# Storing attention operands whole and splitting them after the load, with one row spread moved from DRAM to the tensor engine

## The chip, the cores and the metric

The kernel runs on one core of a Trainium2 chip. The metric is the device time of one execution in microseconds (us). Before the change the median of three runs was 2708.47 us (2705.57 to 2710.37).

A core has TensorE (matrix products, transposes), VectorE (DVE), ScalarE (ACT) and GpSimd (POOL), each with its own queue worked off in order, and SyncE (SP), whose queue issues nearly all transfers here. The transfers themselves run on 16 DMA engines. PEld is TensorE's loading of weights.

## The reference

An encoder of two layers over 1024 tokens of width 1024, all in float32. In each layer one input projection feeds four groups of four heads, whose outputs are joined, projected and added to `x`; then comes an MLP with squared ReLU.

```
proj = rms_norm(x, norm1_g) @ w_in                       # split into the inputs of A, B, C, D
A: q = rms_norm(cq) @ w_uq ; c = rms_norm(ckv) ; k, v = c @ w_uk, c @ w_uv    # rotary part of 32, shared key
   o = softmax(q k^T * 96**-0.5) v                        # dense, 4 heads
B: w = softmax(q1 k1^T) - lam * softmax(q2 k2^T) ; o = rms_norm(w v)          # dense, 4 heads
C: o = softmax(q k^T / 8 over |i - j| <= 128, with sink) v                    # banded, 4 heads on 2 key heads
D: o = softmax(q k^T / 8 + bias over 8 rows x 16 columns) v                   # neighbourhood, 4 heads
x = x + concat(norm(A), B, norm(C), norm(D)) @ w_out
x = x + square(relu(rms_norm(x) @ w_up)) @ w_down
```

## The kernel before

Activations are held transposed: 8 tiles of 128 features by 1024 tokens. To keep float32 accuracy from products of the reduced type `fp32r`, an operand is **split** into a high part (a ScalarE copy to `fp32r`) and a low part (the operand minus the high part, on VectorE or GpSimd; `split`, line 190 for the subtraction, 196 for the copy). A product then takes three matmuls: high by high, high by low, low by high (lines 222 to 224).

A layer's attention (`attention`) goes in order through B, D, C and A, with other work woven in by `weave`: beside B run the latent projections (`proj_latent`) and D's projections (`proj_d`); beside D run C's projections (`proj_c`) and then the second step of the latents (`latent_up`), which gives A's queries, keys and values; beside C and A runs the first half of the output projection. An order of priorities is written out this way, and a planner with a simulated timeline turns it into each engine's queue; on the chip each queue then runs in order.

Between a projection and its attention all operands go through DRAM. A projected half tile (128 features by 512 tokens) comes out of PSUM into a buffer `part` (three of them), scaled by the norm's reciprocals; rotary tiles (`ev_rope`) take two such buffers, D's (`ev_grid`, which reorders the tokens into column blocks) take two per tile. `emit_parts` then splits it into `both` (two buffers, high and low side by side), by ScalarE and by VectorE or, from the second tile of B on, GpSimd, and SP stores both parts. Values (`to_values`) are first transposed by TensorE, and the split reads PSUM: ScalarE copies the high part and VectorE subtracts.

The attention loads what it needs into `stack` buffers (128 by 1024; eight share one pool) and values into `v` (two buffers, `vtile`, high and low side by side, so that one matmul gives both products). B puts high, high and low parts of a query on 3 x 32 partitions against high, low, high of the key, so that one matmul does the three products. D and C put the high and the low part of the query on the two halves of the partitions, against a stack with the key's high part twice and one with its low part twice. A has four stacks a head: high and low, of query and key, each of 64 plain and 32 rotary rows. Softmax takes score tiles from PSUM on VectorE (lines 812, 1058, 1089: add bias or mask, negate, running minimum), then an exponential on ScalarE into `p` tiles (six buffers), then transposes (846, 991), another split into `pth` and `ptl`, and the products with `v` (834, 835, 1003, 1004). The denominators' reciprocals are turned into a row by a transpose, stored to DRAM (`drows`, `rows_of`), and loaded back spread over the partitions (`rz`, `spread`); GpSimd or VectorE multiplies.

The reciprocal norms of the latents go the same way: `proj_latent` ends with `rows_of`, and `latent_up` begins with two `spread` loads, into `rq` and `rkv`. Elsewhere, `spread_here` makes such a spread without DRAM: for each 128 tokens a matmul of the broadcast column with the identity (line 299), and a VectorE copy out of PSUM (294).

D's bias table has six blocks of 128 keys a head: three for a query block inside, and three for the edges, where no column mask on one side is needed.

Of the kernel before, what the change touches and what calls it, by code (L numbers as in the profile page):

```python
# [78 lines left out]
def neighbours():  # L79

    a = np.arange(P)
    q, k = a[:, None], a[None, :]
    r, c, rk, ck = q // 8, q % 8, k // 8, k % 8
    start = np.clip(r - 4, 0, 8)
    row_ok = (rk >= start) & (rk <= start + 7)
    out = np.full((P, 6, P), -1)
    for slot, ok in enumerate((row_ok & (ck >= c), row_ok, row_ok & (ck < c), row_ok, row_ok, row_ok)):
        at = (rk - r + 7) * 31 + 8 * (slot % 3 - 1) + ck - c + 15  # L90
        out[:, slot] = np.where(np.broadcast_to(ok, (P, P)), at, -1)
    return out
# [55 lines left out]
class Trunk:  # L148
# [232 lines left out]
    def attention(self, l):  # L381
# [208 lines left out]
    def ev_rope(self, tabs, dst):  # L590

        dst = dst.rearrange("a g f h s -> a (g f) h s")

        def ev(n, ps):
# [6 lines left out]
            self.tt(t1, t1, t2, ALU.add, self.eng)  # L601
            self.emit_parts(t1, [(dst[:, :, h, sl].rearrange("a p s -> p a s"), slice(h * 64, h * 64 + 64))
# [31 lines left out]

    def to_values(self, dst, tag="mm"):
# [3 lines left out]
        def then(n, y):  # L639
# [6 lines left out]
            nc.scalar.activation(v[..., 0:64], src, AF.Copy)  # L646
            self.tt(v[..., 64:128], src, v.bitcast(F)[..., 0:64], ALU.subtract)
            self.keep(dst[:, :, n * 4:n * 4 + 4].rearrange("h p k e -> p h (k e)"), b.bitcast(F))
# [16 lines left out]
    def proj_latent(self, l, one, xs, rb, tabs, lat, krd, rows_out):  # L665
# [10 lines left out]
        def ev(n, ps):  # L676
# [18 lines left out]
        rows_out.append(self.rows_of(self.rsqrt_cols(both, 192)))  # L695
        yield True

    def latent_up(self, l, lat, rows, qa, ka, va):
        nc, d = self.nc, self.d
        rq, rkv = self.big_tile(F, "rq"), self.big_tile(F, "rkv")  # L700
        self.spread(rq, rows[0], 0, 2)
        self.spread(rkv, rows[0], 1, 2)
# [32 lines left out]
        yield from two(w1[2:3], parts[2:3], plain(rkv, kn[:, 0]))  # L735
# [3 lines left out]
        yield from two([w1[0], both(w1[1])], parts[0:2], plain(rq, qn[:, 1]))  # L739
        yield from two(w1[3:4], parts[2:3], plain(rkv, kn[:, 1]))  # L740
# [190 lines left out]
    def attn_a(self, l, qa, kn, krd, va, ys):  # L931
# [3 lines left out]
        def head(h):  # L935
# [563 lines left out]
```

## Time and profile before

| | |
|---|---|
| Median of three runs | 2708.47 us (2705.57 to 2710.37) |
| The profiled execution's own time | 2709.95 us |
| Its span, first to last instruction | 2707.9 us |
| TensorE busy | 2549.6 us, 94% |
| VectorE, ScalarE, GpSimd busy | 1943.0, 1439.8, 1130.9 us (72, 53, 42%) |
| Mean granted TensorE clock | 0.969 |
| DMA | 389.19 MB in 186931 packets, 144 GB/s on average |

Attention takes roughly the first 650 us of each layer, the MLP the rest. Busy time counts an instruction from its start to its end; the granted clock is the share of full speed at which TensorE was let run. A group of instructions is shown as output and inputs by the program's names, shape, count, then busy time and mean of one in ns, then the idle time of its engine just before and what ended it. Helpers put many operations on one line (190, 196), so the names tell them apart.

### The profile page before, as it was taken

The page shows a single profiled execution, that of the slowest core. Times are in us where ns is not written, and L with a number is a line of the kernel's source. Part 1 is how long each engine was busy: PE and PEld are TensorE (multiplying, and loading weights), DVE is VectorE, ACT ScalarE, POOL GpSimd, SP SyncE. Part 2 cuts the span into 40 slices and gives each one's busy share as a digit, 9 for nine tenths or more (in the row PEclk, how much of TensorE's full clock was granted, in tenths as well). Part 3 has the DMA queues.
Part 4 walks back from the last instruction along what each step waited for, and adds up shares of the span by engine and source line. Part 5 has one row for each costly group of instructions (what it writes and reads, how often), then busy time and mean ns, then how long its engine had stood idle before and what let it go on. Part 6 is the DMA issues. An engine that isn't in the chain of part 4 may idle for free.

```text
span 2707.9 us, 37502 instructions
## 1 busy us (share of the span) xinstructions
PE 2549.6 (94%) x12296; PEld 2112.5 (78%) x12296; DVE 1943.0 (72%) x3379; ACT 1439.8 (53%) x2601; POOL 1130.9 (42%) x754
## 2 busy tenths in 40 slices
PE   8989988999899998999999999889998999999997
PEld 6778876787778887888877788668876788878886
DVE  6777866774966668887567777677749666688775
ACT  4667756664534444444436776566635344444444
POOL 2555642201345554545434656321013455544442
PEclk9989988999999999999998899899999999999998
DMA  5534597222144457444244446962221444664431
GB/s 175 169 107 129 158 287 239 82 89 63 46 144 148 153 170 267 143 142 141 95 139 134 121 113 183 295 202 69 71 71 52 154 153 152 221 221 146 136 105 63
DMA packets 186931, 389.19 MB, mean 144 GB/s; under 512 B 23712, under 2 KB 26736, under 8 KB 186736
## 3 DMA queue, kind: packets, MB, share of 16 engines
q1 hardware_dynamic: 172912, 361.62, 43.2%
q10 hardware_dynamic: 13824, 25.17, 2.7%
q8 instruction: 97, 1.59, 0.2%
q14 instruction: 98, 0.80, 0.1%
HBM read 263.29 MB, written 123.41 MB: 143 GB/s over the span
## 4 chain that ended last, share of the span: by engine, by line
PE 73%; DVE 12%; DMA 6%; ACT 4%; issue 3%; POOL 1%; SPq 0%; DVEq 0%; ACTq 0%; POOLq 0%
PE u L222 8%; PE u L224 8%; PE u L223 8%; PE mm L222 5%; PE mm L223 5%; PE mm L224 5%; PE p L222 5%; PE p L223 5%; PE p L224 5%; PE sb L810 3%; PE tr L846 3%; DVE p L812 2%; DVE part L190 2%; PE pv L835 2%; PE pv L834 2%
## 5 line engine op out<-in xcount | busy, mean ns | idle before, releaser
L190 POOL TENSOR_TENSOR wl<-raw,wh 128x512 fp32r<-128x512 f32 x448 | 632.8, 1413 | 704.8 <-ACT wh L196 691.0
L196 ACT ACTIVATE wh<-raw 128x512 fp32r<-128x512 f32 x448 | 281.5, 629 | 576.2 <-PE u L223 310.9
L190 POOL TENSOR_TENSOR wl<-ws,wh 128x512 fp32r<-128x512 f32 (+1 forms) x112 | 147.3, 1316 | 461.0 <-ACT wh L196 436.1
L222 PE MATMUL u<-far,wh 128*128 128x512 f32 x768 | 301.8, 393 | 11.4 <-ACT ev L1242 8.3
L224 PE MATMUL u<-far,wl 128*128 128x512 f32 x768 | 300.6, 391 | 2.2 <-POOL wl L190 2.2
L190 DVE TENSOR_TENSOR raw<-raw 128x512 f32<-128x512 f32 x256 | 223.1, 877 | 109.1 <-POOL wl L190 55.6
L223 PE MATMUL u<-far,wh 128*128 128x512 f32 x768 | 300.6, 391 | 0.0
L190 DVE TENSOR_TENSOR ptl<-tr,pth 128x512 fp32r<-128x512 f32 (+2 forms) x384 | 238.3, 629 | 68.5 <-ACT pth L196 66.8
L815 ACT ACTIVATE p<-p,nm 128x1024 f32<-128x1024 f32 x192 | 220.2, 1147 | 92.3 <-DVE nm L812 91.6
L196 ACT ACTIVATE pth<-tr 128x512 fp32r<-128x512 f32 (+2 forms) x384 | 205.2, 546 | 108.5 <-PE tr L846 64.9
L222 PE MATMUL p<-far,wh 128*128 128x512 f32 x640 | 252.9, 395 | 7.5 <-DVE ev L190 7.5
L224 PE MATMUL p<-far,wl 128*128 128x512 f32 x640 | 251.5, 393 | 1.5 <-POOL wl L190 1.5
L223 PE MATMUL p<-far,wh 128*128 128x512 f32 x640 | 252.2, 394 | 0.0
L810 PE MATMUL sb<-stack 96*128 96x512 f32 x640 | 217.5, 422 | 22.1 <-DVE nm L812 21.4
L190 DVE TENSOR_TENSOR far<-act,far 128x512 fp32r<-128x512 f32 x224 | 207.3, 955 | 14.7 <-ACT far L196 14.7
L190 POOL TENSOR_TENSOR p<-p 128x1024 f32<-128x1024 f32 x64 | 154.0, 2411 | 129.6 <-ACT p L898 121.3
L222 PEld LDWEIGHTS u<-far,wh 128*128 128x128 f32 x768 | 145.3, 189 | 43.5 <-ACT ev L1242 9.1
L222 PE MATMUL mm<-xh,wh 128*128 128x512 f32 x416 | 170.9, 411 | 0.8 <-DVE part L190 0.3
L224 PEld LDWEIGHTS u<-far,wl 128*128 128x128 f32 x768 | 145.2, 189 | 33.5 <-POOL wl L190 3.0
L812 DVE CUSTOM_DVE_ANT_0 p<-sb,zero,nm 128x512 f32<-128x512 f32 x192 | 142.4, 743 | 37.7 <-PE sb L810 34.6
L223 PEld LDWEIGHTS u<-far,wh 128*128 128x128 f32 x768 | 145.4, 189 | 30.0
L223 PE MATMUL mm<-xl,wh 128*128 128x512 f32 x416 | 167.7, 403 | 0.0
(245 smaller groups left out, 6110.1 us busy)
## 6 DMA issues: line engine op xcount, KB each, us to landing
act<-acts SPq DMA_DIRECT2D x224, 256.0 KB
raw<-in_w_up SPq DMA_DIRECT2D x128, 256.0 KB
acts<-ev SPq DMA_DIRECT2D x128, 256.0 KB
raw<-in_w_down SPq DMA_DIRECT2D x128, 256.0 KB
acts<-ev ACTq DMA_DIRECT2D x96, 256.0 KB
ws<-in_w_in SPq DMA_DIRECT2D x76, 256.0 KB
rz<-drows SPq DMA_DIRECT2D x40, 256.0 KB
stack<-kd SPq DMA_DIRECT2D x32, 256.0 KB
```

The lines of the kernel that those rows point to most:

```text
L190: (eng or self.nc.vector).tensor_tensor(out=out, in0=a, in1=b, op=op)
L196: nc.scalar.activation(hi, src, AF.Copy)
L222: mm(ps, w[0], x[0][:, sl], start=start, stop=False)
L223: mm(ps, w[0], x[1][:, sl], start=False, stop=False)
L224: mm(ps, w[1], x[0][:, sl], start=False, stop=stop)
L810: self.nc.tensor.matmul(ps, q[:, qt * P:(qt + 1) * P], k[:, sl], start=i == 0, stop=i == len(passes) - 1)
L812: self.nc.vector.tensor_tensor_reduce(out=p[:, sl], in0=ps, in1=self.zero[:, 0:1].bitcast(F).broadcast_to([P, 512]), scale=-scale, scalar= ...
L815: self.nc.scalar.activation(p, p, AF.Exp, bias=nm[:, 1:2], scale=-1.0, accum_out=z)
L834: nc.tensor.matmul(out, v[:, kt], h[:, sl], start=kt == 0, stop=False)
L835: nc.tensor.matmul(out, v[:, kt], lo[:, sl], start=False, stop=kt == 7)
L846: nc.tensor.transpose(t[:, k * 256 + i * P:k * 256 + (i + 1) * P], p[:, (j * 2 + k) * P:(j * 2 + k + 1) * P], self.ident)
```

## The change

The operands of A, C and D, except the queries of C and D, are stored as they are, in half the bytes, and so are all values; B's queries and keys are stored split as before.

- `to_whole` stores the `part` buffer of a plain tile; `ev_rope` does the same where its target has no axis for the two parts; `proj_latent` stores the shared rotary key from its buffer.
- `to_values` copies the transposed values out of PSUM on ScalarE into a `part` buffer and stores that. `vtile` loads the whole values into half of a `p` buffer and splits them into `v`.
- `split_here` splits a loaded stack: ScalarE copies the high part to a second stack, VectorE subtracts in place. A splits the query and the key of each head (96 by 1024), D each head's key and C each key head's key (128 by 1024). The number of stacks does not change.
- `proj_latent` keeps the latents' reciprocals as a column; `latent_up` spreads them with two `spread_here` calls.
- D's bias table has five blocks; the query blocks at the edges read two blocks that are two apart.

```diff
-    out = np.full((P, 6, P), -1)
-    for slot, ok in enumerate((row_ok & (ck >= c), row_ok, row_ok & (ck < c), row_ok, row_ok, row_ok)):
-        at = (rk - r + 7) * 31 + 8 * (slot % 3 - 1) + ck - c + 15
+    out = np.full((P, 5, P), -1)
+    for slot, (off, ok) in enumerate(((-1, row_ok), (-1, row_ok & (ck >= c)), (0, row_ok),
+                                      (1, row_ok & (ck < c)), (1, row_ok))):
+        at = (rk - r + 7) * 31 + 8 * off + ck - c + 15
...
-        qb, kb, vb = dr([2, 2, 4, 16, 2, S], "qb"), dr([2, 2, 4, 16, 2, S], "kb"), dr([4, P, 8, P], "vb")
-        qd, kd, vd = dr([2, 2, P, S], "qd"), dr([2, 2, P, S], "kd"), dr([4, P, 8, P], "vd")
-        qc, kc, vc = dr([2, 2, 2, 32, 2, S], "qc"), dr([2, 2, 32, 2, S], "kc"), dr([2, P, 8, P], "vc")
-        lat, krd = dr([2, 3, P, S], "lat"), dr([2, 16, 2, S], "krd")
-        qa = dr([2, 2, P, S], "qan"), dr([2, 4, 16, 2, S], "qar")
-        ka, va = dr([2, 2, P, S], "kan"), dr([4, P, 8, P], "va")
+        qb, kb, vb = dr([2, 2, 4, 16, 2, S], "qb"), dr([2, 2, 4, 16, 2, S], "kb"), dr([4, P, 8, 64], "vb")
+        qd, kd, vd = dr([2, 2, P, S], "qd"), dr([2, P, S], "kd"), dr([4, P, 8, 64], "vd")
+        qc, kc, vc = dr([2, 2, 2, 32, 2, S], "qc"), dr([2, 32, 2, S], "kc"), dr([2, P, 8, 64], "vc")
+        lat, krd = dr([2, 3, P, S], "lat"), dr([16, 2, S], "krd")
+        qa = dr([2, P, S], "qan"), dr([4, 16, 2, S], "qar")
+        ka, va = dr([2, P, S], "kan"), dr([4, P, 8, 64], "va")
...
-                yield from one(T_DK[t], xs, self.ev_grid(rb, self.to_parts(kd[:, t])))
+                yield from one(T_DK[t], xs, self.ev_grid(rb, self.to_whole(kd[t])))
...
+            if whole:
+                for h in range(2):
+                    self.keep(dst[:, h, sl], t1[h * 64:h * 64 + 64])
+                return
             self.emit_parts(t1, [(dst[:, :, h, sl].rearrange("a p s -> p a s"), slice(h * 64, h * 64 + 64))
...
+    def to_whole(self, dst):
+
+        def then(n, y):
+            self.keep(dst[:, n * 512:n * 512 + 512], y)
+        return then
...
-            src = ps.rearrange("p (k h d) -> p h k d", k=4, h=2)
-            b = self.both()
-            v = b.rearrange("p h (k e) -> p h k e", k=4)
-            nc.scalar.activation(v[..., 0:64], src, AF.Copy)
-            self.tt(v[..., 64:128], src, v.bitcast(F)[..., 0:64], ALU.subtract)
-            self.keep(dst[:, :, n * 4:n * 4 + 4].rearrange("h p k e -> p h (k e)"), b.bitcast(F))
+            v = self.part()
+            nc.scalar.activation(v.rearrange("p (h k d) -> p h k d", h=2, k=4),
+                                 ps.rearrange("p (k h d) -> p h k d", k=4, h=2), AF.Copy)
+            self.keep(dst[:, :, n * 4:n * 4 + 4].rearrange("h p k d -> p h (k d)"),
+                      v.rearrange("p (h e) -> p h e", h=2))
...
-            self.emit_parts(y[64:112], [
-                (krd[:, :, h, sl].rearrange("a p s -> p a s"), slice(64 + 32 * h, 80 + 32 * h))
-                for h in range(2)], slice(64, 112))
+            for h in range(2):
+                self.keep(krd[:, h, sl], y[64 + 32 * h:80 + 32 * h])
...
-        rows_out.append(self.rows_of(self.rsqrt_cols(both, 192)))
+        r = self.col("rlat", 16)
+        nc.vector.tensor_copy(r, self.rsqrt_cols(both, 192))
+        out.append(r)
...
-        self.spread(rq, rows[0], 0, 2)
-        self.spread(rkv, rows[0], 1, 2)
+        self.spread_here(rq, rows[0][:, 0:8])
+        self.spread_here(rkv, rows[0][:, 8:16])
...
-        plain = lambda r, dst: self.ev_plain(r, self.to_parts(dst))
-        yield from two([w0[2], both(w0[3])], parts[0:2], plain(rq, qn[:, 0]))
+        plain = lambda r, dst: self.ev_plain(r, self.to_whole(dst))
+        yield from two([w0[2], both(w0[3])], parts[0:2], plain(rq, qn[0]))
...
+    def split_here(self, hi, v):
+
+        self.nc.scalar.activation(hi, v.bitcast(F), AF.Copy)
+        self.tt(v, v.bitcast(F), hi.bitcast(F), ALU.subtract)
+
     def vtile(self, src):
+
         v = self.ap.tile([P, 8, P], R, tag="v", bufs=2, name="v")
-        self.load(v.bitcast(F), src)
+        raw = self.ptile()[:, 0:512].rearrange("p (k d) -> p k d", k=8)
+        self.load(raw, src)
+        self.split(v[..., 0:64], v[..., 64:128], raw)
         return v
...
-            for nope, rope in (((qn[0, t], qr[0, h])), (kn[0, t], krd[0]),
-                               (qn[1, t], qr[1, h]), (kn[1, t], krd[1])):
-                s = self.stack()
+            for nope, rope in ((qn[t], qr[h]), (kn[t], krd)):
+                hi, s = self.stack(), self.stack()
                 self.load(s.bitcast(F)[0:64], nope[h2 * 64:(h2 + 1) * 64])
                 self.load(s.bitcast(F)[64:96], run(rope))
-                tl.append(s[0:96])
-            qh, kh, ql, kl = tl
+                self.split_here(hi[0:96], s[0:96])
+                tl += [hi[0:96], s[0:96]]
+            qh, ql, kh, kl = tl
...
                     self.load(qs.bitcast(F)[half], qd[i, t, rows])
-                    self.load(ks[0].bitcast(F)[half], kd[0, t, rows])
-                for i in range(2):
-                    self.load(ks[1].bitcast(F)[i * 64:(i + 1) * 64], kd[1, t, rows])
+                    self.load(ks[1].bitcast(F)[half], kd[t, rows])
+                self.split_here(*ks)
...
-                    b0 = {0: 4, 7: 3}.get(i, 0)
-                    w = ps.shape[1]
+                    near = bias[:, {0: slice(2, 5, 2), 7: slice(0, 3, 2)}.get(i, slice(1, 4))]
+                    blocks = lambda t: t.rearrange("p (a b) -> p a b", b=P)
...
-                        out=p, in0=ps, in1=bias[:, b0:b0 + w // P].rearrange("p a b -> p (a b)"),
+                        out=blocks(p), in0=blocks(ps), in1=near,
...
-            for n, k in enumerate(ks):
-                for i in range(2):
-                    self.load(k.bitcast(F)[i * 64:(i + 1) * 64], run(kc[n, kv]))
+            for i in range(2):
+                self.load(ks[1].bitcast(F)[i * 64:(i + 1) * 64], run(kc[kv]))
+            self.split_here(*ks)
```

More of the change, by code (lines that the diff above doesn't have):

```diff
@@ L590, in ev_rope @@
     def ev_rope(self, tabs, dst):
-        dst = dst.rearrange("a g f h s -> a (g f) h s")
+        whole = len(dst.shape) == 4
+        dst = dst.rearrange("g f h s -> (g f) h s" if whole else "a g f h s -> a (g f) h s")
         def ev(n, ps):
@@ L663, in latent_parts, with proj_latent @@
                         slice(0, rows), g[:rows])
-    def proj_latent(self, l, one, xs, rb, tabs, lat, krd, rows_out):
+    def proj_latent(self, l, one, xs, rb, tabs, lat, krd, out):
         nc = self.nc
@@ L731, in latent_up @@
         yield from two([w0[0], both(w0[1])], parts[0:2], self.ev_rope(tabs, qr))
-        plain = lambda r, dst: self.ev_plain(r, self.to_parts(dst))
-        yield from two([w0[2], both(w0[3])], parts[0:2], plain(rq, qn[:, 0]))
+        plain = lambda r, dst: self.ev_plain(r, self.to_whole(dst))
+        yield from two([w0[2], both(w0[3])], parts[0:2], plain(rq, qn[0]))
         w1 = self.weights(d["w_lat"][l, 1])
-        yield from two(w1[2:3], parts[2:3], plain(rkv, kn[:, 0]))
+        yield from two(w1[2:3], parts[2:3], plain(rkv, kn[0]))
         w2 = self.weights(d["w_lat"][l, 2])
@@ L738, in latent_up @@
             yield from two(w2[t:t + 1], parts[2:3], self.ev_plain(rkv, self.to_values(va[2 * t:2 * t + 2])))
-        yield from two([w1[0], both(w1[1])], parts[0:2], plain(rq, qn[:, 1]))
-        yield from two(w1[3:4], parts[2:3], plain(rkv, kn[:, 1]))
+        yield from two([w1[0], both(w1[1])], parts[0:2], plain(rq, qn[1]))
+        yield from two(w1[3:4], parts[2:3], plain(rkv, kn[1]))
     def stack(self, dt=R):
@@ L1040, in attn_d @@
                 h = 2 * t + h2
-                bias = self.ap.tile([P, 6, P], F, tag="bias", bufs=1, name="bias")
+                bias = self.ap.tile([P, 5, P], F, tag="bias", bufs=1, name="bias")
                 self.load(bias, self.d["bias"][l, h])
@@ L1069, in attn_c @@
         nc = self.nc
-        mask = self.ap.tile([P, 6, P], F, tag="bias", bufs=1, name="mask")[:, 0:3]
+        mask = self.ap.tile([P, 5, P], F, tag="bias", bufs=1, name="mask")[:, 0:3]
         self.load(mask, self.d["swa"])
```

## The prediction

> **What bounds the kernel now.** I read the page first, then stretches of the span, then the chain of waits and the queue of transfers inside the stretches that stood out. The page gives the span, TensorE's share, its granted clock and the share of the 16 DMA engines, each row in 40 slices of 67.7 us.
>
> ```profile
> span 2707.9 us, 37502 instructions
> PE   8989988999899998999999999889998999999997
> PEclk9989988999999999999998899899999999999998
> DMA  5534597222144457444244446962221444664431
> ```
>
> TensorE is busy nearly everywhere, so a transfer, or work on another engine, counts only where TensorE stands. Two places have low digits in the rows PE and PEclk and a 9 in the row DMA at once: slices 6 and 7 (from 340 us, layer 0) and slices 26 and 27 (from 1690 us, layer 1). Both are where neighbourhood attention (D) ends, windowed attention (C) runs, and the latent projection fills in. The view of stretches (busy us and instructions of PE, PEld, DVE, ACT, POOL, then granted clock, DMA share, GB/s) makes it sharp:
>
> ```profile
> 200.00:300.00 100.00, 99.03 (x555) 84.48 (x555) 77.28 (x204) 76.39 (x125) 53.80 (x30) 1.00 0.46 135
> 336.00:460.00 124.00, 103.66 (x559) 86.58 (x558) 82.64 (x218) 79.42 (x206) 42.30 (x28) 0.91 0.92 280
> 500.00:600.00 100.00, 96.07 (x601) 83.27 (x600) 76.63 (x171) 66.11 (x117) 12.33 (x8) 1.00 0.31 90
> 1676.00:1800.00 124.00, 102.64 (x545) 85.86 (x543) 78.61 (x208) 77.06 (x199) 42.72 (x28) 0.90 0.94 278
> ```
>
> In differential attention (B, 200 to 300) and latent attention (A, 500 to 600) TensorE is busy 96 to 99% at full clock. In the two stretches of 124 us it stands 20.3 and 21.4 us, and runs at 0.91 and 0.90 when busy, while the DMA engines are full to 0.92 and 0.94. At full clock its work there would take 103.66 x 0.91 = 94.3 us and 102.64 x 0.90 = 92.4 us. So each stretch loses about 30 us, the largest loss that this change can touch. The chain of waits (start, length) says what the time goes to:
>
> ```profile
> 352.60 9.21 DMA rq<-drows
> 361.82 10.88 DMA latp<-lat
> 412.38 8.37 DMA va<-both
> 430.24 2.84 DMA qan<-both
> 442.74 7.37 DMA rz<-drows
> 450.27 2.35 POOL y L190
> ```
>
> Transfers of 256 and 512 KB stand on the chain one after the other, 3 to 11 us each: the spread reciprocals `rq`, the latents `latp`, the stores of values and queries. The one `rz` (the softmax denominators) is not touched by the change, only its neighbours on the queue are.
>
> **The change part by part.** *Bytes.* Whole tensors are half as large as high and low part together, stored and loaded. Sizes and counts (both layers) from the view of transfers, and the first and last stores of that work on SP's queue:
>
> ```profile
> qan<-both SPq DMA_DIRECT2D x8, 512.0 KB
> kan<-both SPq DMA_DIRECT2D x8, 512.0 KB
> va<-both SPq DMA_DIRECT2D x8, 512.0 KB
> qar<-both SPq DMA_DIRECT2D x8, 256.0 KB
> kc<-both SPq DMA_DIRECT2D x8, 256.0 KB
> vc<-both SPq DMA_DIRECT2D x4, 512.0 KB
> stack<-kc SPq DMA_DIRECT2D x16, 256.0 KB
> v<-vc SPq DMA_DIRECT2D x4, 512.0 KB
> rq<-drows SPq DMA_DIRECT2D x2, 512.0 KB
> rkv<-drows SPq DMA_DIRECT2D x2, 512.0 KB
> 336.35 1.28 SPq L169 DMA_DIRECT2D kc<-both  x2
> 438.60 0.39 SPq L169 DMA_DIRECT2D kan<-both  x1
> ```
>
> Per layer: A's stores 4 x 512 x 3 + 4 x 256 = 7168 KB, halved, save 3.6 MB; C's (4 x 256 + 2 x 512 stored, 8 x 256 + 2 x 512 loaded, 5120 KB) save 2.6 MB; `rq` and `rkv` (1024 KB) vanish. That is 7.2 MB of the 124 us x 280 GB/s = 34.7 MB of the first stretch, without D's keys and values or A's first loads, which save more there. The DMA share falls from 0.92 to at most 0.92 x 27.5 / 34.7 = 0.73, or 91 us of transfers in 124. That is below TensorE's work, so transfers stop being the floor.
>
> *Work removed, moved and added.* Per layer 18 splits at the store vanish (4 of D's keys, 2 of C's, 2 of the shared rotary key, 10 of A's queries and keys); the 14 subtractions behind the value transposes move to the load, where ScalarE also copies once more (14 value tiles); and 14 splits of whole stacks appear (A 8, D 4, C 2). The nearest rows:
>
> ```profile
> L196 ACT ACTIVATE both<-part 128x512 fp32r<-128x512 f32 x56 | 34.9, 627 | 58.1 <-POOL part L190 29.9 <-DVE part L190 14.6 <-DMA qb<-both 6.8
> L190 POOL TENSOR_TENSOR both<-part,both 128x512 fp32r<-128x512 f32 x48 | 64.3, 1342 | 59.9 <-ACT both L196 40.6 <-DVE nb L1089 11.1 <-DMA ws<-in_w_out 3.2
> L199 ACT ACTIVATE xh<-x,par 128x1024 fp32r<-128x1024 f32 x16 | 18.0, 1142 | 2.7 <-DMA x<-in_x 1.5 <-DVE x L190 1.2
> L190 DVE TENSOR_TENSOR y<-y,rz 128x1024 f32<-128x1024 f32 x8 | 11.0, 1399 | 22.0 <-DMA rz<-drows 22.0
> L190 DVE TENSOR_TENSOR both<-mm,both 128x512 fp32r<-128x512 f32 x20 | 13.6, 685 | 0.9 <-ACT both L646 0.7
> L190 DVE TENSOR_TENSOR raw<-raw 128x512 f32<-128x512 f32 x256 | 223.1, 877 | 109.1 <-POOL wl L190 55.6 <-DMA raw<-in_w_up 51.6
> L294 DVE COPY rb<-mm 128x512 f32<-128x512 f32 x8 | 5.5, 688 | 12.2 <-PE mm L299 12.2
> 34.85 1.95 PE L299 MATMUL mm<-ident,rs_r 128*128 128x128 f32 x16
> ```
>
> GpSimd: 18 x 1.342 = 24 us less per layer. ScalarE: 14 x 1.142 + 14 x 0.627 - 18 x 0.627 = 13.5 us more. VectorE: 14 x 1.399 for the stacks, 14 x (0.877 - 0.685) because the values now come from SBUF, and 4 x 0.688 for the spread, 25 us more. TensorE: one spread by matmuls takes 1.95 us (last row), two are added, 3.9 us more per layer; the removed transpose is one matmul, left out.
>
> *Where it lies.* (a) The two stretches. With the transfers no longer full, their floor is TensorE's work with the spread: 94.3 + 3.9 = 98.2 and 92.4 + 3.9 = 96.3 us, so at most 25.8 + 27.7 = 53.5 us can be won. At the least nothing is won, if other waits take the place. I take half, 27 us: of the six pieces of chain above, `rq` goes, `va` and `qan` halve and lie behind a shorter queue, `latp` keeps its bytes but no longer follows the 1 MB of `rq` and `rkv`, and `rz` with the GpSimd product behind it stays. The splits of D's and C's stacks (6 x 1.399 on VectorE, which is busy 82.64 of 124 us there) are inside this half; without that cover they cost 8.4 us per layer.
>
> (b) The start of B, where values are stored and the first heads are loaded:
>
> ```profile
> 80.00:100.00 20.00, 16.57 (x66) 12.92 (x65) 17.39 (x31) 10.72 (x19) 12.26 (x8) 0.81 0.88 255
> 1420.00:1440.00 20.00, 16.90 (x62) 12.93 (x61) 16.84 (x34) 10.86 (x19) 10.22 (x7) 0.76 0.81 236
> ```
>
> TensorE stands 3.4 and 3.1 us and loses 16.57 x 0.19 + 16.90 x 0.24 = 7 us of clock. B's queries and keys keep their bytes; only values halve. Between 0 and 13.7 us, I take 2, since the wait there is for queries, keys and weights.
>
> (c) Latent attention. A head gains two stack splits and a value split: VectorE 2 x 1.399 + 0.877 = 3.7 us, all of it before the head's products, but the loads can run a head ahead as the eight stack buffers hold two heads of four. VectorE goes from 77% busy to some 88%. Bound from below: 0, hidden in VectorE's idle quarter. From above: all of it, 8 heads x 3.7 = 30 us over both layers. Since TensorE there is 96% busy and softmax already goes through VectorE, I take a quarter, 8 us.
>
> (d) The bias table (six slots to five), the copy of the 16 columns, and a step of two slots at the edges: below nothing to speak of, 0.
>
> The sum: -27 - 2 + 8 = **-21 us**. The profiled execution took 2709.95 us (span 2707.9, about 2 around it), 1.5 above the median, so 2689 by its own time and **2687 us** by the median.
>
> One rule of the Trainium skill speaks against the change. The trace has a VectorE product of 128x16 that took 2.30 us in B, and one of 128x8 that took 0.17 us when GpSimd was idle:
>
> ```profile
> 164.09 2.30 DVE L190 TENSOR_TENSOR rs_t<-rs_t,ms 128x16 f32<-128x16 f32 x1
> 459.40 0.17 DVE L190 TENSOR_TENSOR rs_t<-rs_t,ms 128x8 f32<-128x8 f32 x1 [0.32 <-ACT rs_t L253]
> ```
>
> The Trainium skill, "SBUF — State Buffer", section "Who interferes with whom", says that a VectorE instruction with two SBUF inputs and a GpSimd instruction that reads SBUF lock each other out for a whole instruction. The trace agrees with it in these two rows. The 28 new subtractions per layer all have two SBUF inputs; by that rule each meets a GpSimd instruction a third of the time (42.30 of 124) and waits half of 1.342 us, an estimate of 28 x 0.34 x 0.67 = 6 us of VectorE per layer. With a quarter of it uncovered the sum would be 2690 us, without it 2687.
>
> **The rivals.** *Full recovery.* The halves of the chain that I keep were late only because the queue was full; then both stretches go to their floor: -53.5 - 2 + 8, 2661 us. For it: B at 200 to 300 reaches 99% at a share of 0.46. Against it: `rz` waits for GpSimd and a round trip through DRAM even when the queue is short.
>
> *The transfers are covered anyway.* The bytes fall but the waits are of latency, store then load, and the gain of 27 shrinks to what TensorE's 7.8 us and the 8 of (c) cost: near 0, 2703 to 2714 us, say 2708. For it: a 256 KB `qan` store takes 2.84 us where the queue has just emptied. Against it: five transfers on the chain took 7 to 11.
>
> *Slower: stores hold the projection's buffers.* Before, a projected tile in `part` was free as soon as it was split, and the store read from `both`. Now the store reads `part` itself, of which there are three, and a rotary tile takes two, a value tile one more than its source. VectorE writes `part`, in order, so where the store has not landed VectorE waits, and behind it every softmax minimum and low part, and TensorE for those. Before, ScalarE waited so:
>
> ```profile
> ACT both L646 <- DMA kb<-both: 14.8, 6, 3.6
> ```
>
> The wait is 2.5 us at each of six places. The place is the fill beside C, 18 stores per layer (14 of the latents, 4 of C). If each holds VectorE for half of the 2.84 us landing, 18 x 1.4 x 2 = 51 us, and 2687 + 51 = 2738 us. It decides from (21 / 36) = 0.6 us per store on. For it: the latents' tiles come out a few us apart there. Against it: three buffers of half the bytes are as deep as two of the whole, and the queue is shorter.
>
> **How the numbers follow.** The forecast (part of the loss recovered, 2672 to 2702 us) 0.50; full recovery 0.16; covered anyway 0.12; slower by the held buffers 0.22. This kernel's runs let 0.2%, 5.4 us, be told from no change. Faster 0.50 + 0.16 and a little of the middle is 0.67, same 0.11, slower 0.22. The range goes from the full recovery to where the held buffers cost 0.9 us each (32 us): 2656 to 2718 us; the forecast's own is 2672 to 2702.
>
> **What would show it.** Right: in the stretches after 336 and 1676 us a DMA share near 0.7, PE above 0.9 and a clock above 0.95, and no `rq` on the chain; in A, VectorE near 88% and TensorE still at 96%. Wrong: DVE rows of `part` with a DMA store as releaser for more than 20 us; TensorE in A below 94% with `stack` or `hi` subtractions as releaser; or the DMA share down and the two stretches as long as before. What I see least is the order in which the planner will put the new splits on ScalarE's and VectorE's queues: a split put ahead of its data would stop softmax behind it.

## The result and the profile after

The changed kernel takes **2753.51 us** (median of four runs, 2743.82 to 2755.1) against 2708.81 us of the kernel before in the same comparison: a ratio of 1.0159, 95% interval 1.0133 to 1.0185. The change costs some 43 us where 21 were to be won. The profiled execution took 2752.14 us.

The page of the kernel after begins with these rows, to be laid beside the same ones of before; a slice is 68.8 us here.

```profile
span 2750.3 us, 37481 instructions
PE   8999988899899999999999999889998999989997
PEclk9899998999999999999998999989999999999998
DMA  5433475121244447544244334731121444664431
DMA packets 178098, 350.63 MB, mean 127 GB/s; under 512 B 22720, under 2 KB 32880, under 8 KB 177904
```

The bytes went as they should, from 389.19 to 350.63 MB, and the 9 in the row DMA is gone. TensorE's low digits stay. The view of stretches, first of before, then of after, takes D and C together, in layers 0 and 1, then A (first to last exponential). D and C are taken from the last of ScalarE's copies that scale B's second softmax, which is called the end of B's softmax here, to C's last exponential. Its columns are those explained with the prediction.

```profile
335.50:486.30 150.80, 128.24 (x675) 106.26 (x673) 100.24 (x262) 95.41 (x245) 51.11 (x32) 0.90 0.84 253
1674.10:1824.20 150.10, 125.05 (x664) 103.79 (x663) 98.70 (x260) 96.09 (x244) 52.79 (x33) 0.92 0.86 252
488.30:618.20 129.90, 124.42 (x765) 106.62 (x765) 98.46 (x223) 85.26 (x150) 12.33 (x8) 1.00 0.25 73
1826.90:1956.70 129.80, 124.31 (x765) 106.66 (x764) 98.25 (x222) 85.27 (x151) 12.33 (x8) 1.00 0.25 73
```

```profile
348.90:503.10 154.20, 125.31 (x684) 104.90 (x682) 114.00 (x274) 101.09 (x249) 35.44 (x18) 0.90 0.58 164
1706.70:1860.90 154.20, 125.01 (x684) 105.24 (x682) 112.22 (x274) 100.82 (x248) 35.42 (x18) 0.89 0.58 164
508.70:642.60 133.90, 123.49 (x744) 104.14 (x743) 102.16 (x225) 89.59 (x155) 12.30 (x8) 0.99 0.17 51
1866.80:1997.40 130.60, 123.31 (x742) 103.82 (x742) 102.68 (x225) 89.44 (x156) 12.87 (x8) 0.99 0.17 52
```

In D and C the DMA share falls from 0.85 to 0.58, and the stretch gets 3.4 and 4.1 us longer. GpSimd has 16 to 17 us less work there, VectorE 14 more. A is 4.0 and 0.8 us longer. From the first of B's scaling copies to A's last exponential a layer takes 539.0 and 535.2 us instead of 517.1 and 519.1, which is 38 of the 42 us by which the span grew. Half of these 38 lie in B, from the first to the last of its scaling copies (layer 0 before, then after):

```profile
101.10:335.50 234.40, 224.92 (x1205) 189.56 (x1204) 178.80 (x455) 172.00 (x283) 137.88 (x78) 0.97 0.43 123
```

```profile
103.60:348.90 245.30, 237.48 (x1239) 198.40 (x1239) 181.40 (x453) 172.11 (x279) 131.95 (x73) 0.96 0.37 107
```

B is 10.9 us longer here and 8.0 in layer 1; D and C together are 7.5 us longer over both layers, the steps from C to A 7, A 5.

New waits stand in the views of ScalarE's and VectorE's waits of the kernel after (engine, waiter and its line, what it waited for; us in total, times, longest):

```profile
ACT v L197 <- DMA p<-vb: 14.8, 4, 5.1
ACT v L197 <- DMA p<-vd: 6.6, 2, 3.5
ACT stack L808 <- DMA stack<-kd: 4.9, 2, 2.6
```

```profile
DVE v L191 <- ACT v L197: 18.6, 11, 5.1
DVE part L191 <- DMA vb<-part: 16.2, 4, 7.3
DVE stack L191 <- ACT stack L808: 12.2, 10, 3.2
```

ScalarE now stops for values in the middle of the softmax that it serves, VectorE stops behind it, and VectorE stops for the stores of B's values. The place where D begins in layer 0 shows how. First SP's queue and then ScalarE's in the timeline of after, then SP's of before:

```profile
345.38 0.55 SPq L163 DMA_DIRECT2D p<-vd  x1
```

```profile
349.93 0.58 ACT L197 ACTIVATE pth<-tr 128x512 fp32r<-128x512 f32 x1
353.69 0.63 ACT L197 ACTIVATE v<-p 128x512 fp32r<-128x512 f32 x1 [3.18 <-DMA p<-vd]
354.22 0.58 ACT L197 ACTIVATE pth<-tr 128x512 fp32r<-128x512 f32 x1
354.70 0.50 ACT L1081 ACTIVATE p<-p,nb 128x256 f32<-128x256 f32 x1
```

```profile
295.82 0.34 SPq L162 DMA_DIRECT2D v<-vd  x1
```

Before, D's first values were asked for at 295.82 us, 38 us ahead of D. After, they are asked for at 345.38 us, when B is all but done, and the copy of the split stands in ScalarE's queue ahead of a copy for B and of D's first exponential; both wait with it. The raw values go into a `p` buffer, one of six through which all of softmax rotates.

### The profile page after: what moved, and what is told of

The parts are those of the page before. It is cut to its first block, busy times and chain, and to the rows that moved or that the text cites. A ratio compares the mean times of both kernels' runs of the same rounds, so it can differ in the third digit from the quotient of the medians.

```text
span 2750.3 us, 37481 instructions
## 1 busy us (share of the span) xinstructions
PE 2573.2 (94%) x12358; PEld 2123.3 (77%) x12358; DVE 1982.0 (72%) x3415; ACT 1461.8 (53%) x2621; POOL 1081.5 (39%) x718
## 2 busy tenths in 40 slices
DMA packets 178098, 350.63 MB, mean 127 GB/s; under 512 B 22720, under 2 KB 32880, under 8 KB 177904
## 5 line engine op out<-in xcount | busy, mean ns | idle before, releaser
L831 PE MATMUL sb<-stack 96*128 96x512 f32 x640 | 224.4, 431 | 17.8 <-DVE nm L833 13.9
L867 PE MATMUL tr<-ident,p 128*128 128x128 f32 x1024 | 160.2, 278 | 8.0 <-DVE ptl L191 7.1
```

Source lines behind the costliest of these rows:

```text
L831: self.nc.tensor.matmul(ps, q[:, qt * P:(qt + 1) * P], k[:, sl], start=i == 0, stop=i == len(passes) - 1)
L867: nc.tensor.transpose(t[:, k * 256 + i * P:k * 256 + (i + 1) * P], p[:, (j * 2 + k) * P:(j * 2 + k + 1) * P], self.ident)
```

## The experiments

Switches were built into the changed kernel, 1 for after and 0 for before: `VB` for B's values, `VX` for those of D, C and A, `SD`, `SC` and `SA` for the queries and keys ("stacks") that the change stores whole in D, C and A, `SPREAD` for the spread. With 0 the lines of before stand there, split, store and load. All at 1 is the changed kernel. A time is a median, a ratio is to the kernel before in the same runs.

### One part undone, or alone

**values_split**: all values split before the store again.

```diff
-    VB, VX, SD, SC, SA, SPREAD = 1, 1, 1, 1, 1, 1
+    VB, VX, SD, SC, SA, SPREAD = 0, 0, 1, 1, 1, 1
```

> Edit: values are stored and loaded split, as before the change; whole stacks, the spread by the tensor engine and the five-block bias table stay. Theory V (the value split at the load is what costs: ScalarE and VectorE stand at it until the load lands, 27 us of ScalarE's waits for value loads and 18.6 us of VectorE's behind it, and projected values hold `part` until stored, 17.8 us of VectorE's waits): some 30 of the 43 us come back, 2715 to 2725 us. Theory K (the splits of whole stacks are what costs, 7.5 us per layer where D begins and 3.4 where A begins, and their VectorE time in A): little comes back, 2740 to 2750 us. Theory P (any change of the program moves the planner's order, and that is the difference): no rule, within 15 us of 2753 us.

**stacks_split**: all of A's, C's and D's queries and keys split before the store again.

```diff
-    VB, VX, SD, SC, SA, SPREAD = 1, 1, 1, 1, 1, 1
+    VB, VX, SD, SC, SA, SPREAD = 1, 1, 0, 0, 0, 1
```

> Edit: the keys of A, C and D and A's queries are stored and loaded split, as before the change; whole values, the spread by the tensor engine and the five-block bias table stay. Theory V: 2738 to 2748 us, B as long as after the change (245 us in both layers). Theory K: 2715 to 2725 us, the gap from B to D gone, B still longer than before. Theory P: no rule, within 15 us of 2753 us.

**spread_only**: both of these, so that the spread by TensorE and the bias table are left of the change.

```diff
-    VB, VX, SD, SC, SA, SPREAD = 1, 1, 1, 1, 1, 1
+    VB, VX, SD, SC, SA, SPREAD = 0, 0, 0, 0, 0, 1
```

> Edit: only the spread by the tensor engine and the five-block bias table are left of the change; all operands are stored and loaded split. Theories V and K both: the 0.5 MB of each of two spread loads per layer leave the full queue, 3.9 us of TensorE per layer come in, 2695 to 2708 us. Theory P: 2720 us or more is possible.

**spread_dram**: the changed kernel with the spread through DRAM.

```diff
-        self.spread_here(rq, rows[0][:, 0:8])
-        self.spread_here(rkv, rows[0][:, 8:16])
+        self.spread(rq, rows[0], 0, 2)
+        self.spread(rkv, rows[0], 1, 2)
```

> Edit: the latents' reciprocals go through DRAM again, as before the change; whole values, whole stacks and the five-block bias table stay. Theories V and K both: the spread is not the loss, 2750 to 2762 us. If the spread's matmuls were to stand in TensorE's way: 2740 us or less.

Measured: values_split 2717.41 us, ratio 1.0032 (1.0019 to 1.0045). stacks_split 2737.05, 1.0099 (1.0077 to 1.012). spread_only 2709.2, 1.0006 (0.9988 to 1.0024). spread_dram 2734.37, 1.009 (1.0059 to 1.012). So beside the spread whole values cost 28 us, whole stacks 8, both 44; that the spread and the bias table cost anything by themselves is not shown. Undoing the spread in the full change brings 19 us, yet it will be seen to bring nothing once values no longer go through `p`. In spread_dram D's first values are asked for 7 us ahead of B's end instead of 3.5, and ScalarE's waits for B's values fall from 14.8 to 4.2 us, though the edit touches neither. The planner's order of the queues moves with it; which of these moves brings the 19 us is open.

### Values without the softmax buffer

**v_inplace**: the raw values are loaded into the low half of their own `v` tile and split in place. **v_inplace_nostack** and **v_inplace_dram** do the same with `SD, SC, SA` at 0, and with `SPREAD` at 0.

```diff
-        raw = self.ptile()[:, 0:512].rearrange("p (k d) -> p k d", k=8)
-        self.load(raw, src)
-        self.split(v[..., 0:64], v[..., 64:128], raw)
+        lo = v[..., 64:128]
+        self.load(lo.bitcast(F), src)
+        nc.scalar.activation(v[..., 0:64], lo.bitcast(F), AF.Copy)
+        self.tt(lo, lo.bitcast(F), v[..., 0:64].bitcast(F), ALU.subtract)
```

> Edit, against the changed kernel: the whole values are loaded into the low half of their `v` buffer and split there in place, so that the load needs no `p` buffer of the softmax; the same bytes, the same ScalarE copies and VectorE subtractions, the same stores. Theory P6 (the value load waits for one of the softmax's six `p` buffers, goes out up to 50 us later than before, and ScalarE and VectorE stand at the split): the first values of D are issued some 50 us ahead of D again, ScalarE's waits for value loads (27 us after the change) fall under 8 us, and some 25 of the 28 us that whole values cost come back, 2722 to 2732 us. Theory W (the work of the splits, or the stores that hold `part`, is what whole values cost): 2745 to 2755 us.

> Edit: whole values, split in place in `v` as in v_inplace; keys of A, C and D and A's queries stored and loaded split as before the change; spread by the tensor engine and five-block bias table kept. Against stacks_split (2737 us), which differs in the `p` buffer alone. Theory P6: 2705 to 2715 us. Theory W: 2732 to 2740 us.

> Edit: as v_inplace, with the latents' reciprocals through DRAM as before the change. spread_dram was 19 us faster than the changed kernel, spread_only 3 us slower than the kernel before. If the spread by matmuls costs by itself: 15 to 20 us under v_inplace. If its cost was one with late value loads, or an accident of the planned order: within 6 us of v_inplace.

Measured: v_inplace 2738.4 us, 1.0116 (1.0101 to 1.0132); v_inplace_nostack 2717.97, 1.0037 (1.0024 to 1.0051); v_inplace_dram 2737.19, 1.0113 (1.0097 to 1.0129). v_inplace lies between the ranges of its two theories. The `p` buffer is worth 15 us with whole stacks and 19 without, and with it goes what the spread seemed to cost (2738 against 2737). The row of SP's queue in v_inplace:

```profile
304.96 0.56 SPq L164 DMA_DIRECT2D v<-vd  x1
```

D's values are asked for 40 us earlier than after the change, and D's first exponential comes 1.1 us ahead of the end of B's softmax instead of 5.8 behind it. That the way through `p` costs this is shown where TensorE does the spread. With the spread through DRAM it cost nothing (spread_dram 2734, v_inplace_dram 2737), though there too ScalarE stops 3.24 us for D's first values. Late loads alone are thus not the whole cause; why it takes both is open. In v_inplace 31 us of loss remained.

### Bytes added

**extra_dma**: the kernel before with 28 copies of 256 KB from DRAM to DRAM per layer, 7.3 MB, on SP's queue beside `latent_up`.

```diff
                 ev(n, ps)
+                extra()
                 yield True
...
+        def extra():                      # two copies a call, 14 calls
+            for _ in range(2):
+                for c in copies:
+                    self.keep(*c)         # a part of kc into a spare tensor
+                    break
```

> Edit, on the kernel before: 28 copies of 256 KB per layer from one DRAM buffer to another are added to SP's queue while the latents' second step runs, 7.3 MB per layer, as much as the change was worked out to take out of these stretches; nothing reads them. Theory Q (the prediction's: the full DMA queue sets the length of the stretches after 336 and 1676 us): 24 us per layer at the 300 GB/s seen there, 2740 to 2760 us. Theory L (the stretches are as long as their chains of TensorE, VectorE and ScalarE steps, the transfers are mostly covered): under 10 us, 2708 to 2718 us.

Measured: 2754.36 us, 1.0176 (1.0158 to 1.0194), 47 us, 24 per layer. D and C together in layers 0 and 1, and a part of layer 0:

```profile
334.70:504.40 169.70, 129.99 (x672) 107.71 (x670) 104.50 (x262) 97.94 (x246) 51.28 (x32) 0.85 0.85 266
1686.20:1868.80 182.60, 132.33 (x669) 109.13 (x668) 102.30 (x260) 97.22 (x245) 52.87 (x33) 0.80 0.85 251
420.00:440.00 20.00, 6.92 (x21) 5.42 (x22) 7.43 (x15) 5.43 (x12) 3.97 (x3) 0.52 1.01 311
```

With bytes added the transfers do set the length: for 20 us at a share of 1.01 TensorE works 6.92 us. Taking away is not simply the reverse, as the share of 0.58 in a longer stretch shows. The reading is that before the change the stretch stood at the edge, its transfers nearly full and the work of D and C from engine to engine about as long; that it can get shorter at all is seen further down.

### Where the rest of the loss is

Three start from v_inplace. **v_inplace_both**: a whole value tile is stored from a `both` buffer. **vb_split_inplace**: B's values split before the store (`VB` 0). **sa_split_inplace**: A's queries and keys split before the store (`SA` 0). **kcd_whole**: of the whole change only the spread and D's and C's whole keys (`VB, VX, SA` 0).

```diff
-            v = self.part()
+            v = self.both().bitcast(F)[:, 0]
```

> The kernel v_inplace (2738.4 us), with one change: a whole value tile leaves ScalarE in a `both` buffer (two of 512 KB, as before the change) instead of one of the three `part` buffers, and its store reads it there. Theory H (stores hold the projection's `part` buffers): in v_inplace VectorE's `part` waits 14.7 us in 4 places for the store of B's values; these go, and the time falls by half to all of them, to 2723 to 2731 us. Rival (the held buffers lie beside other waits; what is left of the loss is order and work on ScalarE and VectorE): 2735 to 2742, and the wait turns up at another place.

> The kernel v_inplace (2738.4 us), but B's values are split before their store again, 512 KB a tile, and loaded whole with both parts; D's, C's and A's values and all stacks stay as in v_inplace. In v_inplace ScalarE waits 20.0 us in 6 places for B's values (DMA v<-vb) and VectorE 14.7 us for their store. Theory S (the start of B carries what is left of the values' cost): the 9 us that values cost beside before (2718 for whole values alone, in place) go, and some of the 20 that came on top with the stacks: 2718 to 2728. Rival R (D's, C's and A's splits carry it, by ScalarE's and VectorE's queues): 2734 to 2740.

> The kernel v_inplace (2738.4 us), but A's queries, keys and shared rotary key are split before their store again and loaded in two parts; D's and C's keys and all values stay whole. All stacks split at the store gave 2718.0. Theory KA (A's 16 stack splits of 1.06 us ScalarE and 1.32 us VectorE, in a stage where TensorE is 96% busy, carry the stacks' cost): 2716 to 2722. Rival KD (D's and C's 12 splits, put ahead of softmax on ScalarE, carry it; ScalarE waits 5.2 us for stack<-kd and 7.6 for stack<-kc): 2732 to 2740. Half each: 2727.

> The kernel before with the spread by TensorE and only D's and C's keys whole (12 stack splits at the load); all values and all of A as before. Spread alone gave 2709.2, spread with all stacks whole 2717.4. Theory KA (A's splits carry that 8): 2707 to 2711. Rival KD: 2715 to 2719. Theory Q (transfers in D and C set their length; here the fewer bytes come with only 12 of 28 splits): below 2703.

Measured: v_inplace_both 2727.06 us, 1.0081 (1.005 to 1.0111). vb_split_inplace 2722.44, 1.006 (1.0043 to 1.0077). sa_split_inplace 2708.68, 1.0014 (0.9998 to 1.003). kcd_whole 2700.67, 0.9986 (0.997 to 1.0003). So B's values cost 16 us and A's stacks 30; the buffer that the stores of values hold is worth 11, which overlaps with the 16. That is 46 of the 31 left, so something else in the change gains 15. D's and C's whole keys are the difference between sa_split_inplace and v_inplace_nostack, 9 us by the medians, but the two intervals touch; alone, in kcd_whole, no difference from before is shown.

B's values cost at B's start. The first 50 us from 60 us on, in before, after, and vb_split_inplace:

```profile
60.00:110.00 50.00, 45.54 (x190) 36.06 (x190) 35.32 (x59) 23.50 (x40) 27.32 (x17) 0.90 0.80 232
```

```profile
60.00:110.00 50.00, 43.51 (x162) 32.54 (x163) 28.19 (x56) 22.95 (x39) 21.22 (x15) 0.84 0.71 195
```

```profile
60.00:110.00 50.00, 46.26 (x191) 36.16 (x191) 34.54 (x60) 24.05 (x41) 26.48 (x17) 0.90 0.79 237
```

TensorE gets 28 fewer matmuls done there after the change, and all of them back when B's values alone are split early. In v_inplace it gets 160 done there, in v_inplace_both, where only the buffer differs, 181. The row `DVE part <- DMA vb<-part` is missing in v_inplace_both and in vb_split_inplace.

The stretches of sa_split_inplace, D and C, then A (this execution, 2704.33 us, is the fastest of ten):

```profile
341.40:484.70 143.30, 123.37 (x689) 101.84 (x689) 109.43 (x271) 101.82 (x254) 51.36 (x30) 0.95 0.74 211
1678.10:1819.80 141.70, 121.81 (x684) 100.17 (x684) 110.96 (x271) 101.92 (x254) 50.96 (x30) 0.95 0.73 213
487.20:618.20 131.00, 124.92 (x765) 106.53 (x765) 100.41 (x226) 86.39 (x153) 12.32 (x8) 1.00 0.24 66
1822.30:1953.20 130.90, 124.88 (x765) 106.53 (x765) 100.28 (x226) 86.31 (x153) 12.33 (x8) 1.00 0.24 66
```

Here the forecast gain is to be seen: a share of 0.74, a clock of 0.95, and D and C shorter than before by 7.5 and 8.4 us. In v_inplace, which differs in A's whole stacks alone, D and C take 151.0 us in layer 1: there these stacks had covered it.

### A's stacks: store or load

Each of these two leaves A's low parts out of what is computed, to time one side alone. **a_store** is v_inplace with A's queries and keys stored whole, but loaded twice and not split. **a_load** is sa_split_inplace with A's queries and keys stored in two parts, but only the high part loaded, and split.

```diff
                     hi, s = self.stack(), self.stack()      # a_store
-                    self.load(s.bitcast(F)[0:64], nope[h2 * 64:(h2 + 1) * 64])
-                    self.load(s.bitcast(F)[64:96], run(rope))
-                    self.split_here(hi[0:96], s[0:96])
+                    for x in (hi, s):
+                        self.load(x.bitcast(F)[0:64], nope[h2 * 64:(h2 + 1) * 64])
+                        self.load(x.bitcast(F)[64:96], run(rope))
```

```diff
-                for nope, rope in ((qn[0, t], qr[0, h]), (kn[0, t], krd[0]),      # a_load
-                                   (qn[1, t], qr[1, h]), (kn[1, t], krd[1])):
+            for nope, rope in ((qn[0, t], qr[0, h]), (kn[0, t], krd[0])):
...
+                self.split_here(hi[0:96], s[0:96])
```

> v_inplace (2738.4 us) with A's queries and keys stored whole, as there, but loaded twice and not split at the load: 16 ScalarE copies and 16 VectorE subtractions fewer (A's low parts are then not low parts: the split is left out of what is computed). Theory AL (the splits at the load, as work on ScalarE and VectorE and as waits in their order, carry A's 30 us): 2705 to 2713. Rival AS (the store's side: the tile stays in a `part` buffer until its store has landed, and GpSimd no longer does half of the split): 2732 to 2740.

> sa_split_inplace (2708.7 us) with A's queries and keys split and stored in two parts, as there, but only the high part is loaded and split again at the load (16 ScalarE copies and 16 VectorE subtractions more, half of the loads gone; the low parts are then zero: they are left out of what is computed). Theory AL: 2732 to 2742. Rival AS: 2706 to 2714. Both halves at once would stand near 2723.

Measured: a_store 2719.46 us, 1.0046 (1.0029 to 1.0062); a_load 2722.66, 1.0057 (1.0039 to 1.0075). Neither theory alone: against sa_split_inplace the store's side costs 11 us and the load's side 14, together 25 of A's 30; B too is 7 and 2 us longer in v_inplace than in sa_split_inplace, and no run explains that. The two sides lie mainly in different stages. D and C of a_store with its A of layer 0, then A of a_load in both layers:

```profile
344.50:494.40 149.90, 124.20 (x662) 104.25 (x661) 106.90 (x265) 95.44 (x242) 35.58 (x18) 0.87 0.67 177
1689.50:1836.40 146.90, 123.44 (x671) 102.26 (x670) 108.37 (x266) 96.25 (x242) 35.33 (x18) 0.90 0.66 178
496.90:628.20 131.30, 124.93 (x765) 106.54 (x765) 100.80 (x226) 86.62 (x154) 12.37 (x8) 1.00 0.23 66
```

```profile
489.00:625.40 136.40, 128.65 (x765) 108.98 (x765) 106.11 (x230) 89.73 (x158) 12.36 (x8) 0.97 0.17 52
1832.50:1968.20 135.70, 127.32 (x765) 107.45 (x765) 105.44 (x229) 89.52 (x157) 12.34 (x8) 0.99 0.18 52
```

The splits at the load lengthen A: the same 765 matmuls take 136.4 and 135.7 us instead of 131.0 and 130.9, 10.2 us in all, though VectorE is busy only 78%; D and C are some 4 and 3 us longer in a_load too. The whole store leaves A at its 131 us and lengthens D and C by 6.6 and 5.2 us, where the tiles are projected. Why the store's side costs that is open: in a_store no row of VectorE's waits names a store of A's queries or keys, and the clock falls from 0.95 to 0.87 and 0.90. The planner's order with fewer GpSimd instructions (35.58 us of it instead of 51.36) and the later release of `part` remain as candidates, told apart by no run here.

### The parts that gain

**picked**: spread by TensorE, D's and C's keys whole, D's, C's and A's values whole and split in place; B's values and A's stacks as before the change.

```diff
-    VB, VX, SD, SC, SA, SPREAD = 1, 1, 1, 1, 1, 1      # v_inplace
+    VB, VX, SD, SC, SA, SPREAD = 0, 1, 1, 1, 0, 1
```

> Spread by TensorE, D's and C's keys whole, D's, C's and A's values whole (raw value loaded into the low half of its own tile); B's values and all of A's queries and keys split before their store, as before the change. If the costs add (A's stacks 30 us and B's values 16 us of v_inplace's 2738): 2738 - 30 - 16 = 2692 us. Rival (they don't add, since one slack is won once): 2700 us, as with D's and C's keys whole alone, or more.

Measured: **2692.23 us**, 0.9946 (0.9926 to 0.9965), the fastest here, 14 us below the kernel before. The parts add: v_inplace less 30 and less 16 is 2692. Its stretches, D and C, then A (this execution, 2699.79 us, is above the median):

```profile
334.50:485.80 151.30, 127.66 (x689) 106.17 (x688) 112.23 (x271) 102.11 (x254) 51.58 (x30) 0.91 0.70 200
1669.30:1812.40 143.10, 123.99 (x685) 101.12 (x684) 110.25 (x269) 100.80 (x253) 50.04 (x30) 0.94 0.73 210
488.20:619.20 131.00, 124.96 (x765) 106.53 (x765) 100.53 (x226) 86.37 (x153) 12.37 (x8) 1.00 0.23 66
```

In layer 1 D and C are 7.0 us shorter than before, in layer 0 not shorter in this execution.

## Why the prediction was wrong

The whole loss by steps, from the medians of one kernel to the next: 2753.5 after; 2738.4 without the `p` buffer for raw values (15 us); 2708.7 with A's stacks split early again (30); 2692.2 with B's values too (16). By the ratios the three steps are 12, 28 and 18 us. What is then left of the change gains 14 or 15 us.

**The bytes (term a, -27 us).** The mechanism is borne out in part: sa_split_inplace gains 7.5 + 8.4 = 16 us in D and C, picked 7.0 in layer 1 and nothing in layer 0. Their shares of 0.70 to 0.74 look like the prediction's 0.73 by chance: that was for 124 us and with A's bytes halved, and in 124 us from the same place sa_split_inplace has 0.79 and 0.78. In the full change the gain was covered. The step that failed is the lower bound, "At the least nothing is won, if other waits take the place": it puts no price on a stretch that gets longer. D and C became 3.4 and 4.1 us longer, where 27 us were to be won.

**The start of B (term b, -2).** Wrong in sign. The prediction counted bytes there and no buffers; B's whole values cost 16 us. The row of after is 16.2 us of VectorE in four waits for their stores, the longest 7.3. This is the mechanism of the slower rival, **stores hold the projection's buffers**, which the prediction put beside C, on 18 stores a layer, at 51 us. It was found at B's start, on the values, where storing from the other buffer brought 11 us back.

**Latent attention (term c, +8).** Near in size for the load's side: A is 4.0 + 0.8 us longer after the change and 10.2 by a_load, where 8, a quarter of 30, was taken. What the term left out is the other side of the same move, 11 us in D and C.

**The step with no term at all.** The prediction gave the split of values a duration and no place. "The loads can run a head ahead as the eight stack buffers hold two heads of four" speaks of the stacks; the raw values take softmax's own rotating buffers, and the row of before with `v<-vd` at 295.82 us, from which the distance to D could have been read, was not looked up. The prediction's last sentence named the effect, a split ahead of its data that stops softmax behind it, as what it saw least, and gave it no price. With the spread by TensorE it costs 12 to 19 us.

**The durations** were not at fault. The groups of after:

```profile
L191 DVE TENSOR_TENSOR stack<-stack 96x1024 fp32r<-96x1024 f32 x16 | 21.2, 1323 | 5.0 <-ACT stack L808 4.9
L191 DVE TENSOR_TENSOR stack<-stack 128x1024 fp32r<-128x1024 f32 x12 | 19.3, 1605 | 7.4 <-ACT stack L808 7.3
L191 DVE TENSOR_TENSOR v<-p,v 128x512 fp32r<-128x512 f32 x28 | 20.1, 719 | 18.8 <-ACT v L197 18.6
L808 ACT ACTIVATE stack<-stack 96x1024 fp32r<-96x1024 f32 x16 | 16.9, 1055 | 4.9 <-DMA stack<-krd 2.9 <-DMA stack<-qar 2.0
L300 PE MATMUL mm<-ident,rlat 128*128 128x128 f32 x64 | 8.6, 278 | 0.4 <-DVE rq L295 0.4
```

1399 ns was taken for the subtractions of stacks (1323 and 1605), 877 for those of values (719), 1142 for ScalarE's copies (1055), 3.9 us a layer for the spread (4.3).

**The rivals.** Full recovery fell. Covered transfers had the right picture, a lower share and stretches as long as before, and the wrong time, 2708. The slower rival had the sign, 2738. Of the signs that the prediction named, in 124 us from the same place after B the share came out at 0.65 and 0.64 instead of 0.7, TensorE at 80 and 79% instead of over 90%, and the clock at 0.89 and 0.88 instead of 0.95. VectorE in A came to 76% in layer 0 instead of 88%, and TensorE in A to 92% there, below the 94% named. The DVE rows of `part` behind a store are 17.8 us, under the 20 named. The view of TensorE's waits in A of layer 0 after names softmax's minimum and low part, not the subtractions of stacks:

```profile
PE tr L867 <- DVE ptl L191: 3.4, 6, 1.0
PE sb L831 <- DVE nm L833: 3.3, 5, 1.1
```

Both come from VectorE's queue, in which the subtractions now stand too; that those make them late is argued, and only the 10 us of a_load measure it.

**The lock rule.** The prediction weighed the Trainium skill, "SBUF — State Buffer", section "Who interferes with whom", at an estimated 6 us of VectorE per layer. The trace of after has this row for the subtractions of stacks (ns, least, median, most):

```profile
L191 DVE TENSOR_TENSOR stack<-stack x28: 1201/1222/2155, 280.5 to 1939.5; 96x1024 fp32r<-96x1024 f32 x16, 128x1024 fp32r<-128x1024 f32 x12
```

The trace agrees: of the 28, the 12 that ran beside a subtraction or product of GpSimd took 1749 ns on average, the other 16 took 1215. That is 12 x 0.53 = 6.4 us for both layers together; the 28 subtractions of values, 719 ns on average and 670 at the least, add 28 x 0.05 = 1.4. So some 8 of the 12 us that were estimated for both layers are there; as a cause of the loss they are small.

## What to carry to other kernels

When work moves from before a store to after a load, the question ahead of its duration is which buffer the raw data waits in and when that buffer comes free; read in the trace how far ahead the load goes out now, and price what is lost of it. A split placed after a load stands in the queue of the softmax that needs it; here even a VectorE busy only 78% did not hide it. Undoing one part at a time can mislead, since each edit can move the order of the queues: the spread looked like 19 us in one kernel and like nothing in two others. A move of many operands is best priced and tried operand by operand: here the sum lost 43 us, while some of its parts gain 14.

## What the runs showed of the hardware that was not expected

The DMA share of a stretch did not tell what its transfers were worth. Adding 7.3 MB a layer to D and C, at a share of 0.84 and 0.86 before, cost 24 us a layer. Taking the share to 0.58 won nothing while other waits stood there; at 0.74 and 0.73, with A's stacks split early, D and C were 7.5 and 8.4 us shorter.

A VectorE product took about twice as long beside work of GpSimd. B's rotary products, which the change doesn't touch, in before and after:

```profile
L190 DVE TENSOR_TENSOR part<-p,tabs 64x512 f32<-64x512 f32 x32 | 38.9, 1214 | 2.8 <-POOL part L190 2.4
```

```profile
L191 DVE TENSOR_TENSOR part<-p,tabs 64x512 f32<-64x512 f32 x32 | 30.0, 938 | 2.8 <-DMA vb<-part 2.3
```

Their mean falls from 1214 to 938 ns, 8.9 us in all. Before, 20 of the 32 ran beside a subtraction or product of GpSimd and took 1531 ns on average, the other 12 took 686; after, 11 ran beside one (1421 ns), and the other 21 took 686 again. GpSimd's total is not what decides: in v_inplace_nostack it is 1131.5 us, as before the change (1130.9), and the mean is 937 ns; in vb_split_inplace it is 1085.8 us and the mean 1178. The mean is lowest (937 to 997 ns) in the kernels in which VectorE stops for the stores of B's values; that these stops move the products away from GpSimd's work is argued, not shown.
